# Layer 0's expert sum: one-hot combine products against accumulating scatters to DRAM, and weights laid out tile by tile

## The chip, the cores and the metric

The kernel runs on one core of a Trainium2 chip. The metric is the device time of one execution in microseconds (us). Of the kernel before, three runs are known: 1341.01 us in the median, 1338.43 to 1341.41.

## The reference, cut to what matters

A backbone of two layers works on 256 latent tokens and 256 context tokens of width 1024. Each layer has a mixer and then a mixture of 16 experts. In layer 0 all 512 tokens go through the experts, in layer 1 only the 256 latent ones. A token picks one of four groups and two experts in it, so two gates of the sixteen are not zero:

```python
out = jnp.zeros_like(tok)
for e in range(N_EXPERTS):
    hid = jax.nn.silu(tok @ w1[e]) * (tok @ w3[e])
    out = out + gate[:, e:e + 1] * (hid @ w2[e])
...
hc = hc + g2c * f[:n_c].reshape(hc.shape)
h = h + g2 * f[n_c:].reshape(h.shape)
```

`w1[e]` and `w3[e]` are 1024 x 512, `w2[e]` is 512 x 1024, all in float32, so one expert has 6 MB of weights.

## The kernel before, in words

All large products run on TensorE in three passes (`mm3`, L281 to L286): a float32 operand is split into a high and a low part, and high x high, high x low and low x high are added in PSUM. The split of a weight (`split`, L139 to L152) is one copy on ScalarE (whi, L147) and one subtraction on VectorE (wlo, L149), each over half a tile; with `pool=2` the subtraction of both halves runs on POOL.

Weights come in tiles of 1 MB, 128 partitions x 2048 numbers (raw). `load` (L120 to L129) issues one DMA from the SP queue; for w1, for example, a partition gets four rows of 512 numbers, 2 KB each, from four places in DRAM. The raw tiles go round a ring of slots: four always, two more from the attention on until the end of layer 0's experts (L483), three more in layer 1's (L1151). The split tiles go round a second ring, of six. A load is issued when the split of the tile that last held its slot is done, so the SP queue runs ahead of the engines by the length of the ring.

Layer 0's experts (`moe`, L649; `expert`, L1037 on): the router gives each expert 128 slots and fills them with token numbers; unused slots hold a number past the end, for which the indirect DMA moves nothing. For each expert the POOL queue gathers the tokens' rows from DRAM into xg (`gather`, L989), eight TensorE transposes turn them (tsp, L643), and the two hidden products run, 16 x 3 matmuls each of half (h_ps). `g` is silu of the first (ScalarE, L1052) times the second (VectorE, L1053); four more transposes turn it, and the product with w2 (y_ps) runs. ScalarE writes the gated high part yh (L1073) and VectorE the low part yl (L1074).

The rows of an expert are then brought back to the tokens by a product with a one-hot matrix S (VectorE, L749), `combine`, L759: two matmuls (S x yh, L772, and S x yl, L773) for each half row. Token tiles 2 and 3 (the context; 0 and 1 are the latent tokens) are summed in four PSUM banks (acc) over all 16 experts. Token tiles 0 and 1 are visited in turn, every second expert, in a window of two experts (f_ps), and added to an SBUF sum, facc (L777, L779). `combine_prev` (L1032) calls these one expert late: in expert e, after the second half of w1, for the experts up to e - 1. Expert 0 has none, expert 1 has 12 of these matmuls, experts 2 to 15 have 16 each, and 20 are left for the tail: 256 in all. In expert 15, facc times the modulation row g2 is added to h (`add_gated`, L751 to L757).

The tail (`moe0_tail`, L695) adds expert 15's part, normalizes the context tokens, and starts layer 1's projections; it also splits the first retention weights, on POOL. Layer 1's experts (`expert1`, L1466) work on groups, need no one-hot products, and sum in PSUM.

Where the program text leaves it open, a scheduler sets the order of instructions on each queue at build time; `issue_after` holds a part back behind a given instruction. On each engine the order is then fixed.

Of the kernel before, what the change touches and what calls it, by code (L numbers as in the profile page):

```python
# [17 lines left out]
D = 1024  # L18
# [58 lines left out]

class Net:
# [41 lines left out]
    def load(self, key):  # L120
        if key in self.pre:
            return self.pre.pop(key)
        name, idx, k0, kn, c0, cn = key
        w = self.A[name]
        for i in idx:
            w = w[i]
# [196 lines left out]
    def mixer0(self):  # L323
# [3 lines left out]
        with ExitStack() as es0:  # L327
# [5 lines left out]
            with ExitStack() as es:  # L333
# [52 lines left out]
                with ExitStack() as ea:  # L386
# [15 lines left out]
                    for n in range(2):  # L402
                        if n == 0:
                            ws = [self.weight(key(4 * i, 4, 1792, 512)) for i in range(2)]
                        else:
                            ws = []
                            for i in range(2):
                                t = self.raw_tile().rearrange("p (k n) -> p k n", n=512)
                                w_in = A["mixab_w_in"].rearrange("(k p) n -> p k n", p=128)[:, 4 * i:4 * i + 4]
                                nc.sync.dma_start(t[:, :, 0:256], w_in[:, :, 2304:2560])  # L410
                                nc.sync.dma_start(t[:, :, 256:512], w_in[:, :, 0:256])
                                ws.append(self.split(t))
# [236 lines left out]
    def moe(self, layer, NT):  # L649
        nc = self.nc  # L650
        assert layer == 0
        with ExitStack() as es:
            rp = self.pool(es, f"moe_r{layer}", 1)
            psp = self.pool(es, f"moe_tp{layer}", 2, space=PSUM)
            hps = self.pool(es, f"moe_h{layer}", 2, space=PSUM)
            aps = self.pool(es, f"moe_a{layer}", 1, space=PSUM)
# [13 lines left out]
            with ExitStack() as es2:  # L670
                list(after())
                xg = self.experts_setup(layer, NT, R, ep, psp, hps, aps)
            self.overflow(rv, self.facc[:, 0], self.facc[:, 1])
            with ExitStack() as es2:
# [6 lines left out]
                R["weights"]()  # L681
                self.expert(0)
# [12 lines left out]
    def moe0_tail(self, ep, psp, hps):  # L695
# [12 lines left out]
        mm, add = self.combine(2, 15)  # L708
        last = self.norm_scale(2, x[0])
        with after(last):  # L710
            mm, add = self.combine(3, 15)
# [3 lines left out]
        for t in (0, 1):  # L715
            X["acc"].update({(t, n): X["acc"][t + 2, n] for n in range(2)})
        for t in (2, 3):
            last = self.norm_mod(1, t, x[t - 2], xms, psp, *self.xc)
        with after(last):
            for t in (0, 1):  # L720
                self.combine(t, 15)
# [37 lines left out]
    def combine(self, t, e):  # L759
        X = self.X  # L760
        for n in range(2):
            ns = slice(512 * n, 512 * n + 512)
            acc = X["acc"].get((t, n))
            ps = X["psp"].tile([128, 512], F32, tag="tp", name="f_ps") if acc is None else acc
            e0 = X["done"][t]
            for k in range(e0, e + 1):
                S, yh, yl = X["y"][k]
                st = S[:, 128 * t:128 * t + 128]
                win = t not in X["at"]
                first = k == (e0 if win else 0)  # L770
                last = k == (e if win else 15)
                self.nc.tensor.matmul(ps, st, yh[:, ns], start=first, stop=False)  # L772
                mm = self.nc.tensor.matmul(ps, st, yl[:, ns], start=False, stop=last)  # L773
            if win and e < 15:
                f = self.facc[:, t, ns]
                if e0 == 0:
                    self.nc.vector.tensor_copy(f, ps)  # L777
                else:
                    self.nc.vector.tensor_tensor(f, f, ps, ALU.add)  # L779
            elif e == 15:  # L780
                add = self.add_gated(t, n, ps, X["ep"])
        X["done"][t] = e + 1
        return mm, (add if e == 15 else None)
# [209 lines left out]
    def experts_setup(self, layer, NT, R, ep, psp, hps, aps):  # L993
# [3 lines left out]
        self.X = dict(layer=layer, NT=NT, T=128 * NT, R=R, ep=ep, psp=psp, hps=hps, aps=aps, xg=xg, xs=xs, hs={}, per=1,  # L997
                      y={}, done=[0] * NT, keep=2)
        self.X["at"] = at = (2, 3)
        self.X["acc"] = {(t, n): aps.tile([128, 512], F32, name=f"acc{t}{n}") for t in at for n in range(2)}  # L1000
# [31 lines left out]
    def combine_prev(self, e):  # L1032
        for t in self.X["at"]:
            self.combine(t, e - 1)
        self.combine((e - 1) % 2, e - 1)

    def expert(self, e):  # L1037
        nc, X = self.nc, self.X
        layer, NT, ep, psp, hs, R, T = (X[k] for k in ("layer", "NT", "ep", "psp", "hs", "R", "T"))
        gw = R["gw"]  # L1040
        self.e_hid(e, "moe_w1", 1)
        if 0 < e < 15:
            self.combine_prev(e)
# [13 lines left out]
        if e == 15:  # L1057
            for t in range(2):
                for n in range(2):
                    self.add_gated(t, n, self.facc[:, t, 512 * n:512 * n + 512], ep)  # L1060
        self.e_hid(e + 1, "moe_w1", 0)
        S = ep.tile([128, T], F32R, tag="S", name="S", bufs=X["keep"])
        self.onehot(S, NT, R["tokf"][:, e:e + 1])
        yh = ep.tile([128, D], F32R, tag="yh", name="yh", bufs=X["keep"])
        yl = ep.tile([128, D], F32R, tag="yl", name="yl", bufs=X["keep"])
        X["y"][e] = S, yh, yl
# [563 lines left out]
```

## Time and profile before

| | |
|---|---|
| runs | 1341.01 us (1338.43 to 1341.41) |
| the profiled execution's own time | 1339.33 us |
| its span, first to last instruction | 1337.5 us |
| mean granted TensorE clock | 0.978 |
| layer 0's experts (g of expert 0 to g of expert 15) | 345.1 to 671.9 us |
| layer 1's experts (the same) | 1045.4 to 1308.9 us |
| moved by DMA | 332.40 MB in 176151 packets, mean 249 GB/s |

Engines are PE (TensorE matmul), PEld (its weight loads), DVE (VectorE), ACT (ScalarE), POOL and SP (the queue that issues the weight loads). The end of a matmul is modelled, so a matmul's own duration is longer than the step to the next one: a busy PE is read by the steps between starts. "out<-in" names the tiles by the program's names; what stands in brackets is the idle time before an instruction and who ended it.

### The profile page before, as it was taken

Reading aid. Unit: us, or ns where it says so; the run is one execution under the profiler, and the core shown is the slowest. Engines: PE = TensorE matmul, PEld = TensorE weight load, DVE = VectorE, ACT = ScalarE, POOL = GpSimd, SP = SyncE. Lnnn points to the kernel's source line nnn. Section 1 sums busy time; section 2 is a strip of 40 time slices with the busy share of each in tenths; the row PEclk is TensorE's granted clock in tenths of the full one; section 3 lists DMA queues with packets and bytes.
Section 4 is the critical chain, followed back from the end, with each engine's and each line's share of the span. In section 5 each row is a group of like instructions: output and inputs, shape, how many; then the busy total and the mean of one; then the engine's idle time right before and its main releaser. Section 6 shows DMA issues by size and latency. Waiting matters only on the chain. (4 is left out here: it accounts for less than half of the span.)

```text
span 1337.5 us, 19312 instructions
## 1 busy us (share of the span) xinstructions
PE 1253.8 (94%) x7321; PEld 990.3 (74%) x7321; DVE 981.8 (73%) x1659; ACT 760.0 (57%) x1116; POOL 115.3 (9%) x118
## 2 busy tenths in 40 slices
PE   4999999895999999999979999999998899999995
PEld 3777666574778787878758898988887688877673
DVE  4655576767888888888897754544648899888985
ACT  3654566622777777777744423242534678777763
POOL 2010011102000000000050000000003100000020
PEclk8999999997999999999999999999998999999998
DMA  9777672436898888888846455541487999999990
GB/s 332 265 248 250 227 252 90 159 111 239 286 310 300 292 305 292 304 296 302 280 163 226 144 178 173 175 142 64 147 294 261 382 372 358 358 327 332 350 345 9
DMA packets 176151, 332.40 MB, mean 249 GB/s; under 512 B 9027, under 2 KB 30019, under 8 KB 176048
## 3 DMA queue, kind: packets, MB, share of 16 engines
q1 hardware_dynamic: 164704, 305.16, 65.6%
q0 software_dynamic: 8608, 21.49, 4.6%
q10 hardware_dynamic: 2736, 4.41, 1.0%
q8 instruction: 61, 1.00, 0.3%
q14 instruction: 42, 0.34, 0.1%
HBM read 329.55 MB, written 8.44 MB: 253 GB/s over the span
## 5 line engine op out<-in xcount | busy, mean ns | idle before, releaser
L149 DVE TENSOR_TENSOR wlo<-raw,whi 128x1024 fp32r<-128x1024 f32 x465 | 553.4, 1221 | 128.8 <-ACT whi L147 126.9
L147 ACT ACTIVATE whi<-raw 128x1024 fp32r<-128x1024 f32 x476 | 486.4, 1055 | 172.8 <-PE h_ps L286 71.3
L285 PE MATMUL h_ps<-wlo,xh 128*128 128x512 f32 x512 | 206.0, 402 | 5.9 <-DVEq L1534 3.2
L284 PE MATMUL h_ps<-whi,xh 128*128 128x512 f32 x512 | 206.1, 403 | 1.2 <-ACT xh L646 1.2
L286 PE MATMUL h_ps<-whi,xl 128*128 128x512 f32 x512 | 203.8, 398 | 0.0
L285 PEld LDWEIGHTS h_ps<-wlo,xh 128*128 128x128 f32 x512 | 96.8, 189 | 39.1 <-DVE wlo L149 16.0
L284 PEld LDWEIGHTS h_ps<-whi,xh 128*128 128x128 f32 x512 | 97.2, 190 | 21.8 <-ACT xh L646 1.6
L286 PEld LDWEIGHTS h_ps<-whi,xl 128*128 128x128 f32 x512 | 96.9, 189 | 20.8
L245 PE MATMUL ada_ps<-raw,cT 128*32 128x128 f32 x1536 | 54.9, 278 | 1.4 <-DMA raw<-in_ada_w 1.4
L284 PE MATMUL y_ps<-whi,gh 128*128 128x512 f32 x128 | 51.1, 399 | 1.6 <-DVE facc L779 1.6
L284 PE MATMUL y<-whi,gh 128*128 128x512 f32 x128 | 51.6, 403 | 0.7 <-ACT gh L646 0.7
L245 PEld LDWEIGHTS ada_ps<-raw,cT 128*32 128x32 f32 x1536 | 42.2, 111 | 12.7 <-issue 8.7
L286 PE MATMUL y<-whi,gl 128*128 128x512 f32 x128 | 50.8, 404 | 0.8 <-DVE gl L647 0.6
L285 PE MATMUL y<-wlo,gh 128*128 128x512 f32 x128 | 51.2, 400 | 0.3 <-DVE wlo L149 0.3
L286 PE MATMUL y_ps<-whi,gl 128*128 128x512 f32 x128 | 50.7, 396 | 0.4 <-DVE gl L647 0.4
L285 PE MATMUL y_ps<-wlo,gh 128*128 128x512 f32 x128 | 50.6, 395 | 0.0
L989 POOL DMA_INDIRECT xg<-xd,tok x19 | 21.8, 1148 | 286.3 <-PE tsp L643 260.2
L149 POOL TENSOR_TENSOR wlo<-raw,whi 128x1024 fp32r<-128x1024 f32 x11 | 28.8, 2635 | 134.7 <-ACT whi L147 134.7
L284 PE MATMUL qk_ps<-xhi,whi 128*128 128x512 f32 x96 | 39.4, 410 | 0.0
L285 PE MATMUL qk_ps<-xlo,whi 128*128 128x512 f32 x96 | 38.8, 404 | 0.0
L286 PE MATMUL qk_ps<-xhi,wlo 128*128 128x512 f32 x96 | 38.4, 400 | 0.0
L284 PE MATMUL qk_ps<-r_xl,whi 128*128 128x256 f32 x128 | 36.3, 283 | 0.0
(439 smaller groups left out, 2538.0 us busy)
## 6 DMA issues: line engine op xcount, KB each, us to landing
raw<-in_moe_w SPq DMA_DIRECT2D x192, 1024.0 KB, 6.5
raw<-in_ada_w SPq DMA_DIRECT2D x48, 1024.0 KB, 7.4
raw<-in_ret_w_in SPq DMA_DIRECT2D x24, 1024.0 KB, 5.2
raw<-in_mixab_w_in SPq DMA_DIRECT2D x8, 1024.0 KB, 6.2
raw<-in_ret_w_out SPq DMA_DIRECT2D x8, 1024.0 KB, 5.1
raw<-in_mixab_w_out SPq DMA_DIRECT2D x4, 1024.0 KB, 9.5
bias<-in_rpb ACTq DMA_DIRECT2D x12, 256.0 KB, 6.1
g<-mod POOLq DMA_DIRECT2D x6, 512.0 KB, 4.6
```

The source lines that it names most:

```text
L147: self.nc.scalar.activation(hi, r, AF.Copy)
L149: eng.tensor_tensor(lo, r, hi.bitcast(F32), ALU.subtract)
L245: mm = nc.tensor.matmul(ps[32 * j:32 * j + 32, 0:128], self.cT[:, kk, :], raw[:, k, 128 * j:128 * j + 128], start=(kk == 0), stop=(kk == 7 ...
L284: mm(out, lh, rh, start=first, stop=False)
L285: mm(out, lh, rl, start=False, stop=False)
L286: self.mm_last = mm(out, ll, rh, start=False, stop=last)
L989: self.nc.gpsimd.indirect_dma_start(out=x, out_offset=None, in_=xd[:, :], in_offset=bass.IndirectOffsetOnAxis(ap=idx, axis=0), bounds_chec ...
```

## The change

Each expert from 0 to 14 no longer keeps yh, yl and S. Its gated rows y go, from the POOL queue, by one indirect DMA with addition to the rows of their tokens in a DRAM tensor F, which is zeroed before expert 0. Expert 15 keeps the one-hot way, for all four token tiles in the tail. F is read back by SP in four pieces (`add_sum`), multiplied by g2 and added to h: token tiles 2 and 3 in expert 15, tiles 0 and 1 in the tail. The four acc banks of PSUM become a third buffer for transposes, a third for hidden products and two for y. On the host, all large weights are stored tile by tile, in the order in which `load` asks for them, so that each of a tile's 128 partitions has its 8 KB in one piece; two loads of two pieces in the mixer become one load each.

```diff
     def load(self, key):
...
-        t = self.raw_tile().rearrange("p (k n) -> p k n", n=cn)
-        self.ld_last = self.nc.sync.dma_start(t, w.rearrange("(k p) n -> p k n", p=128)[:, k0:k0 + kn, c0:c0 + cn])
-        return t
+        t = self.raw_tile()
+        self.ld_last = self.nc.sync.dma_start(t, self.A[key[0]][TILE_AT[key[0]][key[1:]]])
+        return t.rearrange("p (k n) -> p k n", n=key[5])
...
-            psp = self.pool(es, f"moe_tp{layer}", 2, space=PSUM)
-            hps = self.pool(es, f"moe_h{layer}", 2, space=PSUM)
-            aps = self.pool(es, f"moe_a{layer}", 1, space=PSUM)
+            psp = self.pool(es, f"moe_tp{layer}", 3, space=PSUM)
+            hps = self.pool(es, f"moe_h{layer}", 3, space=PSUM)
+            yps = self.pool(es, f"moe_y{layer}", 2, space=PSUM)
...
                 R["weights"]()
+                nc.gpsimd.memset(self.facc[:, 0], 0.0)
+                for t in range(NT):
+                    nc.gpsimd.dma_start(self.F[128 * t:128 * t + 128], self.facc[:, 0])
                 self.expert(0)
...
+    def add_sum(self, t):
+        V, h = self.nc.vector, self.h
+        f = self.facc[:, t % 2]
+        self.nc.sync.dma_start(f, self.F[128 * t:128 * t + 128])
+        V.tensor_tensor(f, f, self.g2[t // 2], ALU.mult)
+        V.tensor_tensor(h[:, t], h[:, t], f, ALU.add)
...
     def expert(self, e):
...
-        if 0 < e < 15:
-            self.combine_prev(e)
...
-        if e == 15:
-            with self.tc.issue_after(self.mm_last.ins):
-                self.combine_prev(e)
...
+        if e < 15:
+            y = ep.tile([128, D], F32, tag="y", name="y")
+        else:
+            S = ep.tile([128, T], F32R, name="S", bufs=1)
+            self.onehot(S, NT, R["tokf"][:, e:e + 1])
...
+            wts = [self.weight(("moe_w2", (layer, e), 0, 4, 512 * n, 512)) for n in range(2)]
+            for t in (2, 3):
+                self.add_sum(t)
...
+            if e < 15:
+                nc.scalar.activation(y[:, ns], ps, AF.Copy, scale=gw)
...
+        if e < 15:
+            nc.gpsimd.indirect_dma_start(out=self.F[:, :],
+                                         out_offset=bass.IndirectOffsetOnAxis(ap=R["tok"][:, e:e + 1], axis=0),
+                                         in_=y, in_offset=None, bounds_check=T - 1, oob_is_err=False,
+                                         compute_op=ALU.add)
```

In the tail, `add_sum(0)` and `add_sum(1)` stand between the two norms of the context tokens and their transposes.

## Rows read from the trace of the kernel before

**Rows 1.** The page, part 1: busy time, share of the span, instructions.
```profile
PE 1253.8 (94%) x7321; PEld 990.3 (74%) x7321; DVE 981.8 (73%) x1659; ACT 760.0 (57%) x1116; POOL 115.3 (9%) x118
```

**Rows 2.** Busy time by stretch: us, PE, PEld, DVE, ACT, POOL, PEclk, DMA share, GB/s.
```profile
1036.00:1056.00 20.00, 15.77 (x63) 11.75 (x62) 15.26 (x21) 10.31 (x11) 4.97 (x4) 0.91 1.04 388
...
372.00:460.00 88.00, 87.88 (x401) 70.09 (x400) 77.03 (x84) 62.17 (x73) 3.96 (x4) 1.00 0.87 301
...
1057.30:1161.80 104.50, 104.50 (x473) 84.50 (x472) 96.17 (x93) 81.86 (x92) 0.00 (x0) 1.00 1.00 364
1161.80:1308.80 147.00, 143.67 (x617) 109.62 (x617) 129.98 (x138) 102.60 (x120) 10.02 (x3) 1.00 0.93 329
```

**Rows 3.** Timeline of ACT, 320 to 700 us: start, duration; silu of experts 0, 1, 2, 12.
```profile
345.06 0.60 ACT L1052 ACTIVATE g<-h_ps 128x512 f32<-128x512 f32 x1
...
363.40 0.60 ACT L1052 ACTIVATE g<-h_ps 128x512 f32<-128x512 f32 x1 [0.22 <-PE h_ps L286]
...
385.17 0.58 ACT L1052 ACTIVATE g<-h_ps 128x512 f32<-128x512 f32 x1
...
605.74 0.59 ACT L1052 ACTIVATE g<-h_ps 128x512 f32<-128x512 f32 x1
```

**Rows 4.** Groups by line, PE, 392.11 to 612.67 us: count, busy us, mean ns, idle.
```profile
L772 PE MATMUL acc<-yh,S 128*128 128x512 f32 x40 | 15.6, 391 | 0.0
...
L773 PE MATMUL f_ps<-yl,S 128*128 128x512 f32 x40 | 15.6, 389 | 0.0
L643 PE MATMUL tsp<-cst,xg 128*128 128x128 f32 x80 | 10.4, 272 | 0.0
```

**Rows 5.** Timeline of PE, 670 to 735 us: start, duration.
```profile
676.65 0.39 PE L772 MATMUL acc<-yh,S 128*128 128x512 f32 x1
...
680.34 0.66 PE L643 MATMUL tsp<-cst,g 128*128 128x128 f32 x4
...
700.72 1.94 PE L309 MATMUL nT<-cst,xg 128*128 128x128 f32 x8 [6.05 <-DVE xg L298]
```

**Rows 6.** Groups by line, DVE, 392.11 to 612.67 us (columns as in rows 4).
```profile
L1074 DVE SCALAR_TENSOR_TENSOR yl<-y_ps,gw,yh 128x512 fp32r<-128x512 f32 x20 | 14.9, 745 | 0.0
L779 DVE TENSOR_TENSOR facc<-facc,f_ps 128x512 f32<-128x512 f32 x20 | 12.8, 682 | 0.0
...
L749 DVE TENSOR_SCALAR S<-iota,tokf 128x512 fp32r<-128x512 f32 x10 | 4.8, 483 | 0.0
```

**Rows 7.** DMA, 372 to 656 us: packets, MB, share of engines; issues and landing us.
```profile
q1 hardware_dynamic: 41051, 81.52, 82.0%
q0 software_dynamic: 1728, 2.92, 3.8%
...
raw<-in_moe_w SPq DMA_DIRECT2D x77, 1024.0 KB, 5.6
xg<-xd,tok POOLq DMA_INDIRECT x11, 4.4
```

**Rows 8.** Waits of the SP queue, 372 to 680 us: us, times, longest.
```profile
SPq L128 <- DVE wlo L149: 268.3, 82, 9.3
```

**Rows 9.** Tile raw, 1050 to 1320 us: idle before its users, by releaser; landing us.
```profile
  ACT whi L147: 24.7, 23
...
DMA to landing us min/median/max: 5.0/7.5/10.3
```

**Rows 10.** Waits, whole span: us, times, longest.
```profile
PE ada_ps L245 <- DMA raw<-in_ada_w: 1.4, 1, 1.4
```

**Rows 11.** The page, part 5: busy us, mean ns, idle before and its releaser.
```profile
L989 POOL DMA_INDIRECT xg<-xd,tok x19 | 21.8, 1148 | 286.3 <-PE tsp L643 260.2
```

**Rows 12.** Issues over the whole span: the scatters at the end, us to landing.
```profile
out_dram<-hg,tok POOLq DMA_INDIRECT x4, 7.5
```

**Rows 13.** Timeline of DVE, 670 to 735 us: start, duration.
```profile
693.51 2.15 DVE L757 TENSOR_TENSOR h<-h,gtmp 128x512 f32<-128x512 f32 x1
...
712.79 1.28 DVE L756 TENSOR_TENSOR gtmp<-acc,g 128x512 f32<-128x512 f32 x2
```

More of the change, by code (lines that the diff above doesn't have):

```diff
@@ L75, in host_rpb, with weight_tiles, host_tiles, weight_block @@
     return np.ascontiguousarray(out.reshape(NH, 2, 128, 256).transpose(0, 2, 1, 3))
+def weight_tiles():
+    t = {}
+    for n in ("moe_w1", "moe_w3"):
+        t[n] = [((l, e), 4 * i, 4, 0, 512) for l in range(2) for e in range(16) for i in range(2)]
+    t["moe_w2"] = [((l, e), 0, 4, 512 * n, 512) for l in range(2) for e in range(16) for n in range(2)]
+    t["ada_w"] = [((l,), 4 * i, 4, 512 * c, 512) for l in range(2) for c in range(12) for i in range(2)]
+    t["mixab_w_in"] = [((), 4 * i, 4, c, 512) for c in (1792, (2304, 0)) for i in range(2)]
+    t["mixab_w_in"] += [((), 0, 8, c + 256 * g, 256) for g in range(3) for c in (256, 1024)]
+    t["mixab_w_out"] = [((), 4 * i, 4, 512 * n, 512) for n in range(2) for i in range(2)]
+    t["ret_w_in"] = [((), 0, 8, c + 256 * h, 256) for h in range(4) for c in (1024, 0)]
+    t["ret_w_in"] += [((), 4 * i, 4, c + 512 * h, 512) for h in range(4) for c in (2048, 4096) for i in range(2)]
+    t["ret_w_out"] = [((), 4 * k, 4, 512 * n, 512) for n in range(2) for k in range(4)]
+    return t
+TILES = weight_tiles()
+TILE_AT = {n: {t: i for i, t in enumerate(v)} for n, v in TILES.items()}
+def host_tiles(name, w):
+    out = np.empty((len(TILES[name]), 128, 2048), np.float32)
+    for i, (idx, k0, kn, c0, cn) in enumerate(TILES[name]):
+        m = w[idx].reshape(-1, 128, w.shape[-1])[k0:k0 + kn].transpose(1, 0, 2)
+        cs = c0 if isinstance(c0, tuple) else (c0,)
+        out[i] = np.concatenate([m[..., c:c + cn // len(cs)] for c in cs], -1).reshape(128, 2048)
+    return out
+def weight_block(A, name, layer, e, k, n):
+    key = ((layer, e), 0, 4, 512 * n, 512) if name == "moe_w2" else ((layer, e), k - k % 4, 4, 0, 512)
+    return A[name][TILE_AT[name][key], :, 512 * (k % 4):512 * (k % 4) + 512]
 class Net:
@@ L405, in mixer0 @@
                         else:
[L406 to L412, printed above, removed]
+                            ws = [self.weight(key(4 * i, 4, (2304, 0), 512)) for i in range(2)]
                         pss = [mm4.tile([128, 512], F32, tag="mm", name="v_ps") for t in range(4)]
@@ L707, in moe0_tail @@
         xms = lambda: ep.tile([128, 4, 128], F32, tag="g", name="xm")
-        mm, add = self.combine(2, 15)
+        mm, add = self.combine(2)
         last = self.norm_scale(2, x[0])
         with after(last):
-            mm, add = self.combine(3, 15)
+            mm, add = self.combine(3)
         last = self.norm_scale(3, x[1])
@@ L720, in moe0_tail @@
             for t in (0, 1):
-                self.combine(t, 15)
+                self.combine(t)
         v = hps.tile([128, 512], F32, tag="h", name="v_ps")
@@ L757, in add_gated, with combine @@
         return nc.vector.tensor_tensor(h[:, t, ns], h[:, t, ns], tmp, ALU.add)
-    def combine(self, t, e):
+    def combine(self, t):
         X = self.X
+        S, yh, yl = X["y"]
+        st = S[:, 128 * t:128 * t + 128]
         for n in range(2):
             ns = slice(512 * n, 512 * n + 512)
[L763 to L783, printed above, removed]
+            ps = X["psp"].tile([128, 512], F32, tag="tp", name="f_ps")
+            self.nc.tensor.matmul(ps, st, yh[:, ns], start=True, stop=False)
+            mm = self.nc.tensor.matmul(ps, st, yl[:, ns], start=False, stop=True)
+            add = self.add_gated(t, n, ps, X["ep"])
+        return mm, add
+    def add_sum(self, t):
[4 more added lines that the diff above has]
+        V.tensor_tensor(h[:, t], h[:, t], f, ALU.add)
     def route_setup(self, layer, NT, psp):
@@ L996, in experts_setup @@
         xs = self.xs
[L997 to L1000, printed above, removed]
+        self.X = dict(layer=layer, NT=NT, T=128 * NT, R=R, ep=ep, psp=psp, hps=hps, yps=yps, xg=xg, xs=xs, hs={}, per=1)
+        self.F = self.dram.tile([128 * NT, D], F32, name="moe_sum")
         for e in range(len(xg)):
@@ L1067, in expert @@
         for n in range(2):
             ns = slice(512 * n, 512 * n + 512)
-            wt = self.weight(("moe_w2", (layer, e), 0, 4, 512 * n, 512))
-            ps = psp.tile([128, 512], F32, tag="tp", name="y_ps")
+            wt = wts[n] if e == 15 else self.weight(("moe_w2", (layer, e), 0, 4, 512 * n, 512))
+            ps = X["yps"].tile([128, 512], F32, tag="y", name="y_ps")
             for k in range(4):
                 self.mm3(ps, (gh[:, k], gl[:, k]), self.wk(wt, k), k == 0, k == 3)
-            nc.scalar.activation(yh[:, ns], ps, AF.Copy, scale=gw[:, e:e + 1])
@@ L1607, in host_arrays @@
         a[k] = a[k].reshape(s)
+    for k in TILES:
+        a[k] = host_tiles(k, a[k])
     a["rpb"] = host_rpb(a.pop("na_rpb")[0])
```

43 lines of the change are left out of this document (15 added, 28 removed).

## The prediction, made before the change was run

> **What bounds the kernel now.** I read the page's first part, then the stage table, then the stage that the change touches. TensorE is busy 94% of the span [rows 1], but an average over stages does not price a stage. In the stage table, layer 0's experts (372 to 460 us) show PE 87.88 us of 88, DVE 77.03, ACT 62.17, the granted clock at 1.00 and the DMA share at 0.87 [rows 2]. The g rows of ScalarE, one per expert, give the pace: from 385.17 to 605.74 there are ten periods, so 22.06 us per expert, while the very first period, 345.06 to 363.40, is 18.34 us [rows 3]. No combine product stands in that first period (expert 0 has none, expert 1's follow its first g), so the trace already holds one period without the work that the change removes. In ten experts TensorE runs four groups of 40 combine products, of which the first and the last are shown, so 16 in each [rows 4]; the 16 before expert 15's transposes take from 676.65 to 680.34, 3.69 us [rows 5]. So TensorE sets the pace, and the combine is a sixth of it.
>
> **The change part by part.** The sum is made against the profiled execution's 1339.33 us (span 1337.5); the median of the runs, 1341.01, stands 1.7 us above it, and I add that at the end.
>
> *Combine products go.* Of 256, 16 stay (expert 15's); four of those that go stand in the tail and are left to its bounds. Per period 3.69 us of TensorE go, so a pace set by TensorE alone falls to 22.06 - 3.69 = 18.4, which agrees with the 18.34 seen. That is the lower bound of the new period.
>
> *What is late next, VectorE and ScalarE.* In the same ten experts the yl, facc and S rows cost VectorE 14.9 + 12.8 + 4.8 = 32.5 us, 3.2 per expert, and all three go [rows 6]. VectorE's 77.03 us in 88 are 19.3 per expert [rows 2], which leaves 16.1; ScalarE keeps its count (y is scaled where yh was) at 62.17 in 88, 15.6. Both are under 18.4, but close. The nearest rows for three engines that close together are layer 1's experts, with the same 72 weight products: 104.5 us for six, 17.4 each, then 147.0 for eight, 18.4 each, mean 17.96 [rows 2]. Layer 0 has eight more transposes per expert (layer 1 does eight for four experts); ten experts' xg transposes cost 10.4 us [rows 4], of which three quarters, 0.78 us, come on top. So 17.96 + 0.78 = 18.74. I take this value, since it has the small in-order waits in it. The term is 15 periods, experts 1 to 15, x (22.06 - 18.75) = 49.7 us.
>
> *The transfers.* Per expert six 1 MB weight loads and one gather. The queues' rows give their share of the 16 engines: 82.0% for weights, 3.8% for gathers [rows 7], so 18.1 and 0.84 us of each 22.06. In layer 1 the six loads fit into 17.4 us at share 1.00 and 364 GB/s; the share reaches 1.04, at 388 GB/s, when loads queue up [rows 2]. The gather rows' 2.92 MB in 11 gathers are 0.27 MB each: only rows of real tokens move. The scatter adds as many rows again, each added to what lies in DRAM. No row shows an accumulating transfer. Below: it costs what the gather costs, 0.84 us (nothing or a gain is excluded, since bytes are added). Above: three passes over the row (read it, read the sum, write the sum), 2.5 us. Then the transfers need between 17.4 + 0.84 + 0.84 = 19.1 and 18.1 + 0.84 + 2.5 = 21.4 us of share, or, at the 1.04 that the share can reach, 18.4 to 20.6. I take the lower end, as the scatter has the gather's form and size; then the transfers just keep 18.75. The ring of six slots helps: SP waits for VectorE to release slots, not the engines for data [rows 8], and a load lands 5.6 us after its issue [rows 7] where its slot is used some five loads, 15 us, later.
>
> *The layout.* A partition's 8 KB come in one piece instead of four of 2 KB. No row shows that larger pieces are faster per byte: gathers with 4 KB rows spend 3.8% on 2.92 MB, the loads 82.0% on 81.52 MB [rows 7], so gathers are dearer. I price it at nothing in the experts. Layer 1 keeps its time: among the releasers of raw's users, of which the first is shown, no DMA stands, although landing takes 7.5 us [rows 9]. Where TensorE waits for a load, in the prologue, 1.4 us [rows 10], something may come back: 0 to 3, I take 1. As for what the engines can bring at all, 388 GB/s stand over 20 us and 364 over 104.5 [rows 2]. A rule of the Trainium skill speaks against the change here: "DMA: Bandwidth & Descriptors", Specifications, puts the HBM limit of a core at some 358 GB/s. By it an expert's weights, gather and scatter, 6.29 + 0.27 + 0.27 = 6.83 MB, take 19.1 us at the least, and the kernel would end near 1300; the trace does not agree, by its 388.
>
> *New waits on POOL and SP.* A scatter waits for y, and behind it on POOL stands a gather needed more than one expert later; one gather's issue takes 1.1 us [rows 11]. Each scatter must wait for the landing of the one before: 7.5 us for the scatters at the end [rows 12], under 18.75. Cost: nothing; if a landing took 18 us, the chain of scatters would set the pace. The zeroing (one memset, four 0.5 MB writes) comes at expert 0, where a full ring of loads hides it: nothing, and at most 6 us if the engines were already behind (2.1 MB at 364 GB/s).
>
> *The tail.* Sums for tokens 256 to 511 are read back on SP in expert 15, after scatter 14 has landed, with the retention weights' loads queued behind them. VectorE loses two facc adds and the eight half-row operations that put facc into h, and gets eight full-row operations (four add_sum). At 0.64 us per half row (1.28 for two [rows 13]) that is 16 halves for 10, 3.8 us more, and operations on SBUF alone run slower in the first part of the tail (2.15 us for a half row [rows 13]). Bounds: 0 where TensorE's products of expert 15 cover it, 9 where VectorE also waits 5 us for the read-back. I take 4, the operations alone and nothing hidden, since TensorE already waits 6.05 us for VectorE in that stretch [rows 5]; a wait for the read-back stays in the upper bound alone, because the gather's 4.4 us [rows 7] is the only landing of that size nearby, and expert 15's products take longer.
>
> Sum: 1339.3 - 49.7 + 4 - 1 = 1292.6; on the scale of the runs 1294.
>
> **The rivals.** *Transfers become the bound (B).* For: a share of 0.87 before a sixth of the time is taken away, and 1.00 already in layer 1 [rows 2]. Against: landing times far under the ring's reach. At a period of 20.0, between 18.75 and 20.6, the term is 15 x 2.06 = 30.9, so 1313; at 20.6 and with the dear tail, 1327. The Trainium skill ("Collectives: The Full Stack", Part 3, The bandwidth ceiling) says that a reducing transfer has two source reads and runs at half the rate of a copy. By it the scatter costs 1.7 us; no run here shows it.
>
> *The accumulating rows hold the engines up (C), slower.* Place: the same 16 engines that carry the weights, in every expert. The share has room for 22.06 x 1.04 = 22.9 us; less 18.1 and 0.84, 4.0 are left. From a scatter 4.8 times as dear as a gather, layer 0 is slower than before. At eight times, 6.7 us, the period is 25.6 / 1.04 = 24.7, and the kernel ends 39 us later, 1383 with the tail. For: nothing in the trace shows what the addition costs. Against: it is the smallest transfer of the stage.
>
> *Layer 1 gains too (D).* Its last eight experts run at 18.4, its first six at 17.4. If late loads made that difference and the layout mends it, 8 x 0.95 = 7.6 us more go, 1287, and with a period of 18.4 and no cost in the tail 1277. Against: [rows 9] shows no wait for data.
>
> *The change does not do what it says:* the DMAs may be cut into 2 KB pieces as before. Then the SP queue's packets stay at their count; the forecast loses 1 us.
>
> **How the numbers follow.** Chances: forecast (1283 to 1303) 0.56, D 0.08, B 0.22, C 0.10, gain and costs cancelling 0.04. Time 1294, of the likeliest. The range 1277 to 1328 reaches from D's end to B's; C, the cancelling case and the ends beyond are left out. A measurement can tell 0.2%, some 2.7 us, from no change: faster 0.86, same 0.04, slower 0.10.
>
> **What would show it.** Right: g rows 18.5 to 19 us apart, no acc or f_ps products before expert 15, PE near full, DMA share about 1.0, raw landing below 15 us, no ScalarE wait on raw. Step by step: the tail's VectorE rows some 3.8 us longer; fewer, larger packets on SP's queue. Wrong: whi waiting for raw's DMA in layer 0 (B), scatter landing beyond 18 us or a period over 22 (C), layer 1 under 17.5 throughout (D).

## The result, and the profile after

The changed kernel takes 1307.62 us in the median (1306.32 to 1309.31, four runs), beside 1340.24 us for the kernel before on the same chip: a ratio of 0.9759, 95% interval 0.9741 to 0.9776, so 32.6 us faster. The forecast was 1294, in a range of 1277 to 1328. The sign and the place of the gain came as forecast; in the profiled executions about 22 us came back as losses outside the experts, of which the sum had 3. These two executions lie 30.0 us apart (1339.33 and 1309.31 us) and the medians 32.6, so some 2.6 of the 22 us are the choice of executions.

Page of the changed kernel, part 1 (busy us, share, instructions; beside [rows 1]) and part 3 (queue: packets, MB, share of 16 engines):

```profile
PE 1202.9 (92%) x7081; PEld 946.0 (72%) x7081; DVE 944.2 (72%) x1584; ACT 752.0 (58%) x1116; POOL 143.2 (11%) x138
...
q1 hardware_dynamic: 47232, 307.26, 62.5%
```

240 matmuls are gone. The weights' queue moves its 307.26 MB in 47232 packets; the variant with the old layout (experiment 2) has 165280 packets in its page for the same bytes, so the pieces are longer, as the change says.

Busy time by stretch, changed kernel (us, PE, PEld, DVE, ACT, POOL, granted clock, DMA share, GB/s), experts and then a part of the tail:

```profile
372.00:460.00 88.00, 88.00 (x405) 70.98 (x404) 78.48 (x77) 73.39 (x86) 15.31 (x10) 1.00 0.99 375
...
645.00:656.00 11.00, 0.76 (x9) 0.55 (x13) 9.90 (x15) 2.62 (x4) 8.40 (x4) 0.50 0.87 320
```

In the experts TensorE is busy all 88 us and the DMA share went from 0.87 [rows 2] to 0.99: two things are full at once. No wait of an engine from 372 to 622 us names a transfer there, so TensorE still sets the pace. In the tail there are 11 us in which TensorE works 0.76 us and its granted clock is 0.50, the lower level.

Timeline of ScalarE, changed kernel (start, duration; in brackets the idle time before and who ended it): the gates g of experts 0, 1 and 15, the first vh of the projections after them, and the first g of layer 1:

```profile
349.12 0.60 ACT L1059 ACTIVATE g<-h_ps 128x512 f32<-128x512 f32 x1
367.29 0.59 ACT L1059 ACTIVATE g<-h_ps 128x512 f32<-128x512 f32 x1
...
623.71 0.60 ACT L1059 ACTIVATE g<-h_ps 128x512 f32<-128x512 f32 x1 [0.44 <-PE h_ps L315]
...
681.98 0.62 ACT L1244 ACTIVATE vh<-r_v 128x512 fp32r<-128x512 f32 x1
...
1012.38 0.60 ACT L1493 ACTIVATE g<-h_ps 128x512 f32<-128x512 f32 x1 [6.34 <-DVEq L1550]
```

The same three last rows of the kernel before:

```profile
671.87 0.58 ACT L1052 ACTIVATE g<-h_ps 128x512 f32<-128x512 f32 x1
...
721.25 0.62 ACT L1228 ACTIVATE vh<-r_v 128x512 fp32r<-128x512 f32 x1
...
1045.44 0.60 ACT L1477 ACTIVATE g<-h_ps 128x512 f32<-128x512 f32 x1 [2.43 <-DVEq L1534]
```

With expert 0's g at 345.06 [rows 3] before, the two executions divide like this (us):

| stretch | before | after | difference |
|---|---|---|---|
| start to g of expert 0 | 345.06 | 349.12 | +4.1 |
| g of expert 0 to g of expert 15 | 326.81 | 274.59 | -52.2 |
| g of expert 15 to the first vh | 49.38 | 58.27 | +8.9 |
| first vh to layer 1's first g | 324.19 | 330.40 | +6.2 |
| layer 1's first g to the end | 292.06 | 294.92 | +2.9 |

The sum is, up to rounding, the difference of the spans (1337.5 and 1307.3). The marks do not cut the work alike. Before, 36 combine products lie between expert 15's g and the first vh, the 16 of [rows 5] among them; after, 16 do. And 2135 matmuls lie between the first vh and layer 1's first g after, 2064 before. So the third and the fourth row are safer read together: 373.57 us before, 388.67 after, 15.1 more. The mean period from expert 1 to 15 is (623.71 - 367.29) / 14 = 18.32 us. The experiments ask what sets this period now, and where the 22 us of losses come from.

DMA of the changed kernel, 372 to 622 us (queue: packets, MB, share; then issues, KB each, median us to landing; beside [rows 7]):

```profile
q1 hardware_dynamic: 11585, 84.35, 87.7%
q0 software_dynamic: 3660, 6.55, 10.9%
...
raw<-in_moe_w SPq DMA_DIRECT2D x79, 1024.0 KB, 9.7
moe_sum<-y,tok POOLq DMA_INDIRECT x14, 10.6
```

### The profile page after: what moved, and what is told of

The parts are those of the page before. It is cut to its first block, busy times and chain, and to the rows that moved or that the text cites. A ratio compares the mean times of both kernels' runs of the same rounds, so it can differ in the third digit from the quotient of the medians.

```text
span 1307.3 us, 18799 instructions
## 1 busy us (share of the span) xinstructions
PE 1202.9 (92%) x7081; PEld 946.0 (72%) x7081; DVE 944.2 (72%) x1584; ACT 752.0 (58%) x1116; POOL 143.2 (11%) x138
## 3 DMA queue, kind: packets, MB, share of 16 engines
q1 hardware_dynamic: 47232, 307.26, 62.5%
## 5 line engine op out<-in xcount | busy, mean ns | idle before, releaser
L176 ACT ACTIVATE whi<-raw 128x1024 fp32r<-128x1024 f32 x476 | 480.0, 1053 | 101.1 <-PE qk_ps L314 22.1
L1088 POOL DMA_INDIRECT moe_sum<-y,tok x15 | 27.9, 1857 | 153.8 <-ACT y L1083 153.8
L669 ACT ACTIVATE gh<-tsp 128x512 fp32r<-128x512 f32 x32 | 19.1, 596 | 43.4 <-PE tsp L666 43.2
L1541 POOL DMA_INDIRECT out_dram<-hg,tok x4 | 6.6, 1662 | 274.5 <-DVE hg L1535 219.5
```

What stands on the lines that cost most here:

```text
L176: self.nc.scalar.activation(hi, r, AF.Copy)
L669: nc.scalar.activation(hi[:, b0:b0 + w], tv, AF.Copy)
L1088: nc.gpsimd.indirect_dma_start(out=self.F[:, :], out_offset=bass.IndirectOffsetOnAxis(ap=R["tok"][:, e:e + 1], axis=0), in_=y, in_offset=N ...
L1541: self.nc.gpsimd.indirect_dma_start(out=self.out[:, :], out_offset=bass.IndirectOffsetOnAxis(ap=idx, axis=0), in_=x, in_offset=None, bound ...
```

## The experiments

Each ran beside the kernel before; medians of runs, with the ratio's 95% interval. Periods and stretches come from the g and vh rows of ScalarE, as above.

### 1. The layout alone

```diff
 # before, with the tiles stored in the order of the loads; combine as before
+        self.ld_last = self.nc.sync.dma_start(t, self.A[key[0]][TILE_AT[key[0]][key[1:]]])
```

> The kernel before with the new weight layout alone (combine products stay). Theory: 8 KB packets on the SP queue let the small transfers of the POOL queue land later, so that layer 0's first transposes start about 4 us later and layer 1's branch opens about 4 us later; the experts stay at 22.06 us per period (TensorE). So 1343 to 1348, gathers landing in 6 us or more instead of 4.4. Rival: the layout is harmless there and helps the prologue and the loads: 1335 to 1340, gathers landing as before.

Measured: 1339.31 us, ratio 0.9994 (0.9985 to 1.0004): no change, a period of 22.04 as before, and expert 0's g at 344.35. The theory that the layout delays small transfers fell: the gathers from 372 to 656 us land in 4.3 us (4.4 before). The page of this kernel, part 3, and its busy time by stretch:

```profile
q1 hardware_dynamic: 46656, 305.16, 61.1%
```

```profile
372.00:460.00 88.00, 87.90 (x401) 70.14 (x400) 77.06 (x85) 62.32 (x72) 3.97 (x4) 1.00 0.80 295
```

The DMA share falls from 0.87 [rows 2] to 0.80 at nearly the same rate (301 and 295 GB/s), and the time shows that nobody was waiting for it.

### 2. The scatter alone

```diff
 # before, with F, add_sum, the scatters and the new PSUM buffers;
 # load and the host's layout as before (2 KB pieces)
```

> The changed kernel's scatters with the old layout (2 KB pieces). Theory: the transfers still keep up with TensorE at 18.3 to 18.5 us per expert, and what the layout cost at the two starts comes back: 1298 to 1303. Rival: without the larger pieces the 16 engines become the bound (they needed 18.1 of 22.06 us for the weights alone), the period goes to 19.2 or more, ScalarE waits for raw, and the kernel ends at 1312 or later.

Measured: 1319.22 us, ratio 0.9845 (0.9821 to 0.9869). The rival held in its waits and its time; the period, by the g rows of experts 1 and 15 below, stayed a little under its 19.2. These rows, the busy time by stretch, the DMA from 372 to 622 us, and the longest wait of ScalarE for a transfer there (us, times, longest):

```profile
368.22 0.59 ACT L1036 ACTIVATE g<-h_ps 128x512 f32<-128x512 f32 x1
...
634.40 0.60 ACT L1036 ACTIVATE g<-h_ps 128x512 f32<-128x512 f32 x1 [0.44 <-PE h_ps L286]
```

```profile
372.00:460.00 88.00, 85.48 (x387) 68.63 (x386) 75.63 (x75) 69.85 (x83) 14.19 (x9) 0.98 1.02 355
```

```profile
q1 hardware_dynamic: 40560, 80.56, 90.3%
q0 software_dynamic: 3670, 6.58, 10.8%
...
raw<-in_moe_w SPq DMA_DIRECT2D x77, 1024.0 KB, 14.6
```

```profile
ACT whi L147 <- DMA raw<-in_moe_w: 18.8, 13, 3.1
```

The share stands at 1.02, a load lands after 14.6 us, ScalarE waits for weights 13 times, and the mean period is 19.01. Per MB the weights' queue takes 90.3 / 80.56 = 1.121 percent points; in the full change it takes 87.7 / 84.35 = 1.040, 7% less. So the layout is worth nothing alone and 11.6 us on top of the scatter, 9.8 of them between the g of expert 0 and that of expert 15 (284.3 us here).

### 3. Stored tile by tile, moved in 2 KB pieces

```diff
-    out = np.empty((len(TILES[name]), 128, 2048), np.float32)
+    out = np.empty((len(TILES[name]), 128 * 2048), np.float32)   # (k, p, n) inside a tile
...
+        self.ld_last = self.nc.sync.dma_start(t, w.rearrange("(k p n) -> p k n", p=128, n=key[5]))
```

> The changed kernel with each tile still contiguous as 1 MB in DRAM, but stored row block by row block, so that a partition's 8 KB come as four pieces of 2 KB again. Theory (the packet's size decides): within 3 us of the scatter with the old layout, packets of 2 KB, landing of the gathers as there. Rival (the place in DRAM decides): like the changed kernel, 1306 to 1309.

Measured: 1319.16 us, ratio 0.9839 (0.9822 to 0.9855), the time of experiment 2. Waits of ScalarE, 372 to 622 us:

```profile
ACT whi L177 <- DMA raw<-in_moe_w: 17.2, 13, 3.1
```

The length of a piece decides, not that the 1 MB lie together in DRAM.

### 4. A second scatter in each expert

```diff
+            nc.gpsimd.indirect_dma_start(out=self.F2[:, :], ..., in_=y, ..., compute_op=ALU.add)
```

> Every expert from 0 to 14 adds its rows a second time, into a second sum in DRAM that nothing reads (and that is zeroed like the first). Theory: after the change the transfers bound layer 0's experts as much as TensorE does (share 0.99 at 372 to 460 us). Queue 0's gather and scatter together took 10.9% of the 16 engines' time in 372 to 622 us, about 2.0 us per expert, so a second scatter asks for about 0.7 to 1.2 us more: the mean period goes from 18.32 to 19.0 to 19.5 us, and with 2 to 5 us for zeroing the second sum the time to 1320 to 1330 us. Rival: the transfers still have room beside TensorE's 18 us; the period stays under 18.6 us and the time under 1315 us.

Measured: 1344.46 us, ratio 1.003 (1.002 to 1.004); the theory's direction, at twice the upper end of its period (0.7 to 1.2 us more). The mean period is 20.80 us, 2.48 more. The g of experts 1 and 15, busy time by stretch, DMA from 372 to 654 us, and ScalarE's first wait there:

```profile
364.93 0.59 ACT L1061 ACTIVATE g<-h_ps 128x512 f32<-128x512 f32 x1
...
656.09 0.60 ACT L1061 ACTIVATE g<-h_ps 128x512 f32<-128x512 f32 x1 [0.76 <-PE h_ps L315]
```

```profile
372.00:460.00 88.00, 79.77 (x356) 62.59 (x355) 70.06 (x69) 63.57 (x75) 23.41 (x14) 0.98 0.97 348
```

```profile
q1 hardware_dynamic: 11533, 83.96, 78.2%
q0 software_dynamic: 5769, 10.51, 16.9%
```

```profile
ACT whi L176 <- DMA raw<-in_moe_w: 56.2, 33, 3.2
```

Queue 0's share times the period is 3.5 us per expert here and 10.9% x 18.32 = 2.0 with one scatter, so the second scatter adds 1.5 us of the 16 engines' time; if the gather still takes its 0.84 [rows 7], 1.2 are left for the first. A scatter takes 1.2 to 1.5 us, more than the gather. The Trainium skill ("Collectives: The Full Stack", Part 3, The bandwidth ceiling) has a collective that adds run at half the rate of one that copies. An estimate from that, twice the gather's 0.84, is 1.7 us, and the 1.2 to 1.5 here stay under it. The weights take 78.2% x 20.80 = 16.3 us (87.7% x 18.32 = 16.1 with one scatter). So 1.7 of the 2.48 us are transfers' own time; the rest is a lower share, 95.1% for the two queues in place of 98.6%. The two queues' 98.6% leave the transfers next to no room in the changed kernel: 1.1 us more of them per expert made the period 0.7 us longer (experiment 2), 1.7 us more made it 2.5 longer.

### 5. No read-back

The sum of experts 0 to 14 is left out of the output.

```diff
     def add_sum(self, t):
-        ...
+        return
```

> The changed kernel without add_sum: the sum in DRAM is neither read back nor multiplied nor added, so the experts 0 to 14 are missing from the output. Theory: in the tail the read-back holds up the retention weights' loads on SP, which moves POOL's splits onto VectorE's norm, and add_sum for tokens 0 to 255 stands before the context's r_xc; together some 9 to 13 us, so 1295 to 1299. Rival: the tail is longer because all four one-hot sums of expert 15 now come at the end, not because of the read-back: 1303 to 1308.

Measured: 1300.29 us, ratio 0.9695 (0.9679 to 0.9711): the read-back and its VectorE work cost 7.3 us, between the theory's 9 to 13 and the rival's 0 to 5. From expert 15's g to the first vh it takes 51.65 us, and to layer 1's first g 378.70, 10.0 less than in the changed kernel. ScalarE's timeline in this kernel:

```profile
621.84 0.60 ACT L1056 ACTIVATE g<-h_ps 128x512 f32<-128x512 f32 x1 [0.43 <-PE h_ps L315]
...
673.49 0.62 ACT L1241 ACTIVATE vh<-r_v 128x512 fp32r<-128x512 f32 x1
```

How the read-back costs this is seen in four views of the changed kernel. A wait of the SP queue, 372 to 640 us:

```profile
SPq L800 <- DMA moe_sum<-y,tok: 11.7, 1, 11.7
```

Timeline of POOL, 600 to 690 us, and of VectorE, 636 to 690 us:

```profile
638.58 14.82 POOL L178 TENSOR_TENSOR wlo<-raw,whi 128x1024 fp32r<-128x1024 f32 x6 [15.22 <-ACT whi L176]
```

```profile
642.26 4.32 DVE L783 TENSOR_TENSOR h<-h,gtmp 128x512 f32<-128x512 f32 x2
...
651.15 2.26 DVE L210 SCALAR_TENSOR_TENSOR rs_y<-rs_a,rs_y 128x1 f32<-128x1 f32 x1
...
653.70 0.16 DVE L210 SCALAR_TENSOR_TENSOR rs_y<-rs_a,rs_y 128x1 f32<-128x1 f32 x1
...
656.21 1.28 DVE L783 TENSOR_TENSOR h<-h,gtmp 128x512 f32<-128x512 f32 x2
...
660.02 1.22 DVE L801 TENSOR_TENSOR facc<-facc,g 128x1024 f32<-128x1024 f32 x1
```

Waits of TensorE, 620 to 690 us:

```profile
PE nT L338 <- DVE xg L327: 12.8, 2, 12.5
PE v_ps L315 <- DVE r_xc L349: 3.5, 1, 3.5
```

SP stands 11.7 us at the read-back, waiting for the last scatter to land, with the retention weights' loads behind it. So POOL's six splits of these weights run from 638.58 to 653.40 and meet VectorE's chain from the last combine to the norm: the same one-number-per-partition step takes 2.26 us beside POOL and 0.16 once POOL is done, the addition h + gtmp 2.16 and 0.64. Not every step stretches: those with a single tensor as input keep 0.15 us beside POOL, and the products with an input from PSUM (gtmp<-f_ps,g) keep 0.64; the stretched ones read two tensors from SBUF. TensorE waits 12.5 us for that chain (6.05 before [rows 5]), its granted clock falls to 0.50 meanwhile, and 3.5 us more behind the sums for token tiles 0 and 1, which start at 660.02. The next four experiments try these parts one by one.

### 6. The tail's splits without POOL

```diff
-        self.ret_wv = wv = [self.weight(("ret_w_in", (), 4 * i, 4, 2048, 512), 2) for i in range(2)]
-        self.ret_w0 = w0 = self.weight(self.ret_keys(0)[0], 2)
+        self.ret_wv = wv = [self.weight(("ret_w_in", (), 4 * i, 4, 2048, 512)) for i in range(2)]
+        self.ret_w0 = w0 = self.weight(self.ret_keys(0)[0])
```

> The three retention weights that are split in the tail have all their low parts made by VectorE, none by POOL. Theory: POOL's six splits (14.8 us, 638.6 to 653.4 us) stretch VectorE's chain from the last combine to the norm, whose small steps took 1.4 to 2.3 us in place of about 0.2, and so hold back the transposes by some 4 to 6 us; without them the stretch from the last gated product of expert 15 to the first vh falls from 58.3 to 52 to 55 us and the time to 1302 to 1305 us. Rival: VectorE then has the six splits (about 1.2 us each) in its own queue in the same place, and nothing is won: 1306 to 1312 us.

Measured: 1307.42 us, ratio 0.9750 (0.9734 to 0.9766): nothing, although the stretch from g to vh is 56.93 us, 1.3 less. Timeline of VectorE and of TensorE in this kernel:

```profile
642.23 6.89 DVE L178 TENSOR_TENSOR wlo<-raw,whi 128x1024 fp32r<-128x1024 f32 x6
...
652.97 1.23 DVE L801 TENSOR_TENSOR facc<-facc,g 128x1024 f32<-128x1024 f32 x1
...
655.38 0.15 DVE L210 SCALAR_TENSOR_TENSOR rs_y<-rs_a,rs_y 128x1 f32<-128x1 f32 x1
```

```profile
649.77 0.79 PE L792 MATMUL f_ps<-yh,S 128*128 128x512 f32 x1 [6.77 <-DVE gtmp L782]
```

VectorE's small steps are short again, as the theory has it, but the six splits now stand 6.89 us in VectorE's own queue and TensorE waits 6.77 us for what is behind them. The rival's time came. The kernel does not separate the two, though: the scheduler also moved the four operations of the later sums (1.2 us each, from 652.97) into the middle of the norm's chain, so what POOL's stretching alone costs is not shown.

### 7. The read-back from POOL's queue

```diff
-        self.nc.sync.dma_start(f, self.F[128 * t:128 * t + 128])
+        self.nc.gpsimd.dma_start(f, self.F[128 * t:128 * t + 128])
```

> The four transfers that bring the sum back go out from POOL's queue instead of SP's. Theory: SP's wait of 11.7 us for the scatter of expert 14 holds the loads of the retention weights behind it; without it they go out before 622 us instead of at 629.4, TensorE's wait for the transposes (12.5 us) shrinks by 4 to 8 us, and the time falls to 1300 to 1304 us. Rival: the chain scatter, read-back, add, norm alone sets the tail and the weights wait for nothing: 1306 to 1309 us; or POOL's splits, now behind the read-backs on POOL's queue, are as late as before: the same.

Measured: 1315.80 us, ratio 0.9805 (0.9788 to 0.9821), 8 us slower than the changed kernel; neither theory nor rival had that. From g to vh it takes 65.86 us, 7.6 more. VectorE's and TensorE's timelines:

```profile
635.55 1.23 DVE L801 TENSOR_TENSOR facc<-facc,g 128x1024 f32<-128x1024 f32 x1 [8.05 <-DMA facc<-moe_sum]
```

```profile
638.56 1.11 PE L666 MATMUL tsp<-cst,g 128*128 128x128 f32 x4 [9.32 <-DVE g L1060]
```

SP no longer stands at the scatter (its first load of the retention weights goes out at 618.50 us, not 629.44), but the scheduler now put the sum ahead of expert 15's own gate on VectorE. VectorE stood 8.05 us at the read-back and TensorE 9.32 us behind VectorE. The wait for the last scatter has to stand somewhere; in this order, where it reached VectorE, it cost more than on SP's queue.

### 8. The later sums behind the norm

```diff
-        for t in (0, 1):
-            self.add_sum(t)
         for t in (2, 3):
             last = self.norm_mod(1, t, x[t - 2], xms, psp, *self.xc)
         with after(last):
+            for t in (0, 1):
+                self.add_sum(t)
             for t in (0, 1):
                 self.combine(t)
```

> The two read-backs of the first two token tiles, with their products and sums, stand behind the norm of the other two tiles instead of ahead of it. Theory: their four VectorE instructions of 1.22 us no longer hold up r_xc, TensorE's wait of 3.48 us at v_ps goes, and the stretch from the last gate of layer 0 to the first vh falls from 58.3 to 54 to 56 us: 1303 to 1305.5 us. Rival: VectorE is needed right after by these tiles' own combine and norm, and the work only moves: 57.5 us or more, 1306.5 to 1309 us.

Measured: 1302.97 us, ratio 0.9725 (0.9701 to 0.9749), as the theory had it. From g (620.93) to vh (675.83) it takes 54.90 us, and TensorE's wait at v_ps <- r_xc of VectorE is gone from its waits from 618 to 685 us:

```profile
PE nT L338 <- DVE xg L327: 13.4, 1, 13.4
...
PE v_ps L313 <- ACT r_xc L348: 1.1, 1, 1.1
```

The gain reaches past that mark: from g to layer 1's first g it takes 381.86 us, 6.8 less than in the changed kernel (the median gained 4.7). In the changed kernel TensorE, back at work, pauses a second time, and its granted clock is 0.74 and then 0.92 in the two stretches of 5 us from 663.71; here it is 1.00 from 655.93 on.

### 9. The start: fewer loads ahead of the first gather

In the changed kernel TensorE's first transposes of gathered rows wait for the gather. The scheduler had moved one weight load behind SP's wait for the overflow flag. Two edits were tried: a small transfer that needs the router's table, ahead of the third weight, and the same five loads ahead of the flag's wait as in the kernel before.

```diff
 # hold
+        if e == 0:
+            nc.sync.dma_start(self.dram.tile([128, 16], mybir.dt.int32, name="hold"), R["tok"])
         self.e_hid(e, "moe_w3", 0)
 # early
+            self.prefetch([(nm, (0, e), 4 * i, 4, 0, 512) for e, nm, i in
+                           ((0, "moe_w1", 0), (0, "moe_w1", 1), (0, "moe_w3", 0), (0, "moe_w3", 1), (1, "moe_w1", 0))])
             rv = nc.values_load(R["ovf"][0:1, 0:1], min_val=0, max_val=1)
```

> SP writes out a 64-byte-per-row table that is ready only when the gathers can be issued, ahead of the third of layer 0's expert weights, so that fewer weights are in flight when the first gathers start. Theory: the first gather landed 9.5 us after its issue because two loads of 1 MB went out at 324.4 and 324.8 us, 2 us ahead of it (before the change one did); held to 326.6 us, the gather lands 3 to 4 us earlier, expert 0 starts at 345 to 346.5 instead of 349.1 us, and the time is 1303 to 1305 us. Rival: the gather's time goes with the whole load, or the weights come late instead: expert 0 not before 348 us, 1306 to 1310 us.

Measured: 1311.04 us, ratio 0.9775 (0.9759 to 0.9792): no gain, 3.4 us worse than the changed kernel. The edit missed its aim: SP sent two loads at 323.33 and 325.40 us, both still ahead of the gather at 325.54, and TensorE's wait for it stayed at 9.40 us. So it decides nothing; why it is slower than the changed kernel is open.

> The changed kernel, with expert 0's first four weight tiles and expert 1's first one asked for ahead of SP's wait for the overflow flag, as the kernel before has them; in the changed kernel the fifth of these stands behind that wait. Theory: that is why two loads of 1 MB go out at 324.4 and 324.8 us, 2 us ahead of the first gather (326.6), where the kernel before sent one; with one, the gather lands 3 to 4 us earlier, VectorE's step over its branch takes about 4 us again instead of 6.4, expert 0's first gate starts at 345 to 346.5 instead of 349.1 us, and the time is 1303 to 1305 us. Rival: the gather's 9.5 us come from something else in the scatter variants (the zeroing, the state of the queues); expert 0 not before 348 us and the time 1306 to 1309 us.

Measured: 1304.80 us, ratio 0.9723 (0.9696 to 0.9750), as the theory had it; its four runs (1301.55 to 1307.81 us) overlap those of the changed kernel, so the 2.8 us of the medians are not clear of noise, and the traces carry the argument. The changed kernel first, SP's timeline from 323 to 326.4 us (start, time over all, count):

```profile
324.40 1.64 SPq L157 DMA_DIRECT2D raw<-in_moe_w  x2
```

TensorE's timeline in it, 328 to 342 us:

```profile
336.26 1.94 PE L666 MATMUL tsp<-cst,xg 128*128 128x128 f32 x8 [9.48 <-DMA xg<-xd,tok]
```

The kernel early, SP's timeline in the same stretch:

```profile
325.62 0.33 SPq L157 DMA_DIRECT2D raw<-in_moe_w  x1
```

And TensorE's:

```profile
334.10 1.94 PE L666 MATMUL tsp<-cst,xg 128*128 128x128 f32 x8 [6.03 <-DMA xg<-xd,tok]
```

One load less in those 2 us, and the wait goes from 9.48 to 6.03 us. The other kernels agree: from the first gather's issue to these transposes it takes 8.9 to 11.4 us in the ten kernels with two loads in the 2.3 us ahead of it, and 5.7 to 6.2 in the four with one. Expert 0's g follows the gather's issue (327.88) by 18.2 us, as before (18.4, from 326.65) and not 22.5.

### 10. The code's place at layer 1's branch

ScalarE's first g of layer 1 waits 6.34 us on VectorE's branch (2.43 before; the rows stand above). That is 3.9 of the 6.2 us lost between vh and there; VectorE's own idle time before its next step grows as much, from 0.78 to 4.69 us.

```diff
+            for p in range(75):
+                nc.vector.memset(tokf, 0.0)      # in the overflow branch, never executed
```

> 75 instructions of VectorE that are never executed stand in layer 0's overflow branch, so that VectorE's code at layer 1's branch lies as far from its start as in the kernel before (the change took 75 of VectorE's instructions out ahead of it). Theory: VectorE waits at that branch for code to be fetched, and where the code lies decides how long; ScalarE's first gate of layer 1 waited 6.34 us on VectorE's branch (2.43 us before), and with the padding it waits 2 to 3 us again; the time falls by about 4 us to 1302 to 1305 us. Rival: the wait comes from the load on the transfers at that point, or from how the program before it ran; it stays at 5.5 us or more and the time at 1306 to 1309 us.

Measured: 1307.03 us, ratio 0.9755 (0.9727 to 0.9784). ScalarE's timeline, layer 1's first g:

```profile
1010.77 0.60 ACT L1495 ACTIVATE g<-h_ps 128x512 f32<-128x512 f32 x1 [6.49 <-DVEq L1552]
```

The theory fell, as far as counting instructions can put the code back in its place. The numbers are the rival's, but neither of its two causes was tested. A wait for code is not excluded either: in all fourteen traces a packet of an instruction queue (q14) starts 1.2 to 2.1 us ahead of this g. The idle time of this g is 6.05 to 6.70 us in all twelve kernels with the scatter, 2.43 in the kernel before and 2.44 with the layout alone; its cause stays open.

### 11. What gained, together

```diff
 # early and the later sums behind the norm, and in the overflow branch
+            for p in range(128):
+                nc.vector.memset(tokf, 0.0)
```

> The two edits that gained by themselves, together: the weight tiles asked for ahead of SP's wait for the flag, and the first two tiles' read-back sums behind the norm of the other two. With them, 128 never executed instructions of VectorE in layer 0's overflow branch, a second place for VectorE's code at layer 1's branch. Theory: the two gains (2.8 and 4.7 us) lie in different stretches and add up, and the padding changes nothing, as 75 instructions did: VectorE's step over layer 1's branch stays at 5.5 to 6.5 us and the time is 1299 to 1302 us. Rival: the place of the code does count and 75 was another bad one: the step falls to 2.5 us or less and the time to 1295 to 1298 us. Third: the gains overlap, 1302 to 1304 us.

Measured over five rounds: 1297.74 us (1296.65 to 1301.97), ratio 0.9687 (0.9671 to 0.9704), faster than both kernels. The two gains add up to 7.5 us, and 9.9 were measured: the time lies under the theory's range and in the rival's (1295 to 1298), but the rival's sign, a step of 2.5 us or less at the branch, did not come, so the padding did nothing there. Where the other 2.4 us come from is not shown; no run has the two edits without the padding. ScalarE's timeline:

```profile
343.19 0.60 ACT L1061 ACTIVATE g<-h_ps 128x512 f32<-128x512 f32 x1
...
617.82 0.60 ACT L1061 ACTIVATE g<-h_ps 128x512 f32<-128x512 f32 x1 [0.44 <-PE h_ps L315]
...
999.35 0.60 ACT L1497 ACTIVATE g<-h_ps 128x512 f32<-128x512 f32 x1 [6.05 <-DVEq L1554]
```

The experts' stretch is 274.63 us, that of the changed kernel to 0.04 us: what this version gains lies outside it. Layer 1's first g still idles 6.05 us.

## Why the prediction was right, and where it was not

**The combine products and the engines that come next: right.** The term was 49.7 us; the stretch of the 15 periods gave 52.2. Part of that agreement is luck. Only 14 of the 15 periods had products to lose: the first had none, as the prediction itself says (18.34 us before, 18.17 after), and those of expert 15 stand behind its g (676.65 against 671.87). So 14 x (22.06 - 18.75) = 46.3 was the sum to make, and 14 x (22.03 - 18.32) = 52 came. The period came out at 18.32 against 18.75, at the bound that the first period had shown ("18.34 us"). The step "17.96 + 0.78", layer 1's pace with its small waits, was too careful by 0.4 us. VectorE's 78.48 us in 88 are 16.3 per expert (16.1 forecast), ScalarE's 15.3 (15.6).

**The transfers: right in the sum by two errors that cancel.** "I take the lower end, as the scatter has the gather's form and size" failed: the doubled scatter shows 1.2 to 1.5 us, not 0.84, inside the bounds of 0.84 to 2.5. "I price it at nothing in the experts", of the layout, failed too: its 7% per byte are 1.1 us per expert (90.3% x 19.01 = 17.2 in experiment 2, against 16.1), and without them rival B is what happens (19.01, 1319 us, in its 1313 to 1327). As forecast, a load lands within 15 us (9.7) and ScalarE waits for none. The wrong inference was that gathers with longer rows are dearer, so length does not help; a gather differs from a load in more than its rows' length. The rows did hold the warning, a share of 0.87 with a sixth of the time about to go. The Trainium skill ("DMA: Bandwidth & Descriptors", Specifications) states a limit of about 358 GB/s per core, half of a stack's 716. The 375 of the experts' row, in a kernel that runs on one core, pass it.

**New waits on POOL: right.** A scatter lands after 10.6 us (7.5 forecast), under the period, so the chain of scatters sets nothing. The zeroing was priced at nothing; no engine's wait in the changed kernel points to it, and no run leaves it out.

**The tail: the term that was mis-sized.** "I take 4, the operations alone" came out at 8.9, the upper bound of 9, and even that is flattered: the 3.7 us of expert 15's products, booked among the periods, left this stretch, so what was new in it cost some 12.6. What was left to the bound, the wait for the scatter, did happen: 11.7 us on SP. It did not hold VectorE, as the bound had it, but SP's next loads, and through them POOL's splits, which then ran beside VectorE's chain. No read-back at all saves 7.3 us; the order alone, in experiment 8, gives 4.7 back in the median (10.0 and 6.8 in the traces, up to layer 1).

**The prologue and the start: a missing step.** "I take 1" from the layout: it gave nothing clear of noise. The steps had nothing on what the scheduler does with the queues at expert 0; a load that slipped behind SP's wait for the flag explains most of the 4.1 us (the gather is issued at 326.6 us in both kernels; its wait is 3.7 us longer); experiment 9 brought back 2.8 in the median.

**Layer 1 and the stretch before it: another missing step.** "Layer 1 keeps its time" left out the wait on VectorE's branch (3.9 us, cause open). The other 2.3 us of the 6.2 belong to the tail, whose matmuls stand partly behind the first vh: with the order of experiment 8 this stretch is 326.96 us, 2.8 above the kernel before, with the wait at the branch unchanged (6.38). Layer 1's period is 18.05 against 17.97, so rival D, which had it gain, fell. After its last g, the end takes 1.6 us longer, all of it behind the issue of the last scatter of the output (8.4 us to the end before, 10.0 after); nothing here explains it.

**Rival C, slower,** had its turning point at a scatter 4.8 times as dear as a gather; it is 1.4 to 1.8 times as dear. With two scatters per expert the kernel is where C puts it, just slower than before.

## What to carry to other kernels

Price a transfer by what it takes from DMA engines that will be full after the change, not by who waits for it today: the same layout was worth 0 us alone and 11.6 us once the matmuls that hid the transfers were gone. When work moves to a transfer, ask which queue will stand at its landing, and what is queued behind that. Where a scheduler orders the queues, read the new order around each long wait (a flag, a read-back): two slips of order, with what they carried along, cost up to 10 us here and were mended without touching the work.

## What the hardware showed that was not expected

- VectorE's steps that read two tensors from SBUF stretch while POOL splits large tiles: one on a single number per partition took 2.26 us beside POOL and 0.16 after, a 128x512 addition 2.16 and 0.64. Steps with one tensor or with an input from PSUM kept their time.
- ScalarE waited for VectorE at the same branch 2.4 us in the two kernels without the scatter and 6.05 to 6.70 in the twelve with it, whatever stood in the skipped code.
- The granted clock fell to 0.50 in 11 us in which TensorE worked 0.76 us, and was 1.00 through the experts, in which it did not pause.
- One 1 MB load more in the 2 us ahead of a small gather made the wait for it 3.5 us longer (9.48 against 6.03), and fourteen kernels fall into two groups by it.
